# Both products of a convolutional feed-forward layer by one level of Strassen's recursion

## The chip, the core and the metric

The kernel runs on one core of a Trainium2 chip. The core has a matrix engine (PE), a vector engine (DVE), a scalar engine (ACT), a small general engine (POOL), a queue engine that issues transfers (SP), an on-chip memory of 128 partitions (SBUF) and eight accumulation banks of 128x512 float32 values (PSUM), which only PE writes. Each engine works through its own queue in order, and engines wait for each other by semaphores. The metric is the device time of one execution in microseconds (us), the median of three runs.

## The reference

One layer of a sequence model on x of 1024 tokens by 1024 features, in float32: a token mixer with two recurrences, then a gated feed-forward part, then a final norm. The change lies in the feed-forward part:

```python
def conv_ffn(h, up_w, conv_w, conv_b, down_w):      # h (1024, 1024), up_w (1024, 5632), down_w (2816, 1024)
    u = causal_dwconv(h @ up_w, conv_w, conv_b)      # causal convolution of width 3 along the tokens
    gate, val = jnp.split(u, 2, axis=-1)
    return (jax.nn.silu(gate) * val) @ down_w
...
x = x + gate_m * token_mixer(...)
h = rms_norm(x, ffn_norm_w) * (1.0 + scale_f) + shift_f
x = x + gate_f * conv_ffn(h, ...)
return rms_norm(x, final_norm_w)
```

## The kernel before

**Precision.** Each float32 operand of a large product is split into two parts of a shorter format, hi and lo (ACT copies hi, DVE subtracts to get lo), and a product is three matmuls: hi by hi, hi by lo, lo by hi. One matmul has a 128x128 stationary operand and 512 moving columns.

**The feed-forward part** keeps h transposed on chip (`hi_T`, `lo_T`: features on the partitions, 8 slabs of 128, by 1024 tokens). The 2816 hidden features are 22 slabs `f` of 128. `up_pair(f)` (L1182) makes one slab of the gate and one of the value: `feat_half` (L263) runs 24 matmuls (8 slabs of the inner dimension, 3 each) into one bank for 512 tokens, so a slab pair has 4 times 24 = 96 matmuls. Then ACT reads the bank twice (L1193: times the last tap, plus bias; L1194: a plain copy), DVE adds the other two taps (L1196), and `glu` (L1210) makes silu(gate)*value and splits it into hi and lo (L1216, L1218), which stay in SBUF. `down(gi)` (L1247) multiplies the slabs of a group of two or three (`GROUPS`) by their rows of `down_w`: for each of 8 token tiles 6 matmuls a slab, added to x in SBUF by DVE (L1270). Groups of ups and downs alternate; after the last group `final` (L1232) applies the final norm and writes the output.

**The order of the work** is written by the program itself: `run(gen)` steps a generator that issues PE work, a tick for every few matmuls, and `spawn` and `later` put the other engines' work a given number of ticks later; every queue then holds that order. Weights come through `Stream` (L155): SP loads 512 KB items into 4 raw buffers (`wraw`), ACT and DVE split them into 4 buffers each of `whi` and `wlo`, `ahead` keeps four items split and four loaded in front of the one in use.

**Before it**, the mixer runs its projections through `tok_block` (L242) and `feat_block`; HGRN2 heads (`hgrn_side`) share elementwise work between DVE and POOL. The last projection, `plan["out", n]` for the two halves n of the features, adds the gated result to x (`o_evac`, L1121), and in the second half `h2_tail` (L1148) makes h for one token tile at a time: POOL's power for the norm (L150), DVE's scaling (L1156), 8 transposes on PE (L379), the modulation on ACT and DVE, hi and lo.

Of the kernel before, what the change touches and what calls it, by code (L numbers as in the profile page):

```python
# [30 lines left out]
GROUPS = [2, 3, 3, 3, 3, 3, 2, 3]  # L31
# [25 lines left out]
def trunk(ctx, tc, x, c, ada_w, ada_b, mix_norm_w, in_w, in_b, mlstm_conv_w, mlstm_conv_b,  # L57
# [11 lines left out]
    vp = ctx.enter_context(tc.tile_pool(name="vp", bufs=1))  # L69
# [85 lines left out]
    class Stream:  # L155
# [24 lines left out]
        def split_hi(self):  # L180
# [4 lines left out]
            _, k, n, gain, work = self.items[i]  # L185
            t = self.raw.pop(i)[:, :k * n]
            if work is not None:
                work(t.rearrange("p (k n) -> p k n", k=k))
                return lambda: None
            if gain is not None:  # L190
                DVE.tensor_mul(t, t, gain())
# [50 lines left out]
    def tok_block(items, evac, ncols=512, before=None):  # L242
        segs = [(0, 512)] if ncols == 512 else [(0, 264), (264, 264)]
        for t in range(NT):
# [4 lines left out]
            for k in range(KD):  # L249
# [6 lines left out]
                if k % 2 == 1 and t == NT - 1:  # L256
                    st.after(items[k // 2], DEFER * (k // 2))
# [67 lines left out]

    def plan_heads(kind, hs):
# [18 lines left out]
    order, groups = [], []  # L345
    f0 = 0
    for gsz in GROUPS:
        groups.append(list(range(f0, f0 + gsz)))
        f0 += gsz
    for gi, fs in enumerate(groups):  # L350
        order += [("up", f) for f in (fs if gi == 0 else fs[1:])]
        if gi + 1 < len(groups):
            order.append(("up", groups[gi + 1][0]))
        order.append(("down", gi))
    for kind, i in order:
        if kind == "up":
            plan["ug", i] = feat_item(upw, i * P)
            plan["uv", i] = feat_item(upw, DFF + i * P)
        else:
            for f in groups[i]:  # L360
                plan["dn", f] = st.add([(0, D, downw[f * P:(f + 1) * P, :].unsqueeze(1))], 1, D,
                                       lambda: gates["f"])
# [172 lines left out]
    with tc.tile_pool(name="start", bufs=1) as sp:  # L535
# [6 lines left out]
        big = [vp.tile([P, 2, 2048], F32, name=n) for n in ("so", "v")]  # L542
# [87 lines left out]
        v_first = vp.tile([P, NT, 4, 129], F32, name="v")  # L630
# [338 lines left out]
    def mix_round(g, kind, v, prev_fin):  # L969
# [40 lines left out]
        so = R["so"] = vp.tile([P, NT, 512], F32, name="so")  # L1010
# [106 lines left out]
    x1h = [vp.tile([P, NT, 512], F32, name="v"), None]  # L1117
# [3 lines left out]
    def o_evac(n):  # L1121
        def sq(t, xt):
            ACT.activation(xt[:, 512:1024], x1h[n][:, t, :], AF.Square, accum_out=ss1[:, n, t:t + 1])

        xts = {}

        def xload(t):
            xts[t] = hdt([P, 1028], "pre" if t % 2 else "acc")
            SP.dma_start(out=xts[t][:, :512], in_=x2d[t * P:(t + 1) * P, n * 512:n * 512 + 512])

        def f(t, ps):
            if t == 0:
                xload(0)
            if t + 1 < NT:
                xload(t + 1)
            xt = xts[t]
            xv = x1h[n][:, t, :]
            DVE.tensor_mul(xv, ps[0], gates["m"][:, n * 512:n * 512 + 512])
            POOL.tensor_tensor(out=xv, in0=xv, in1=xt[:, :512], op=OP.add)
            if n == 0:  # L1140
                later(3, sq, t, xt)
            else:
                spawn(h2_tail(t, xt, sq), 3)
        return f

    h2_done = set()

    def h2_tail(t, xt, sq):  # L1148
        sq(t, xt)
# [4 lines left out]
        xn = hdt([P, 2 * S], "q")  # L1154
        for n in range(2):
            DVE.tensor_scalar(xn[:, n * 512:n * 512 + 512], x1h[n][:, t, :], rs1[:, t:t + 1], None,  # L1156
                              op0=OP.mult)
        yield H2[2]
        d = hdt([P, KD, P], "row" if t % 2 else "kt")
        modulate(t, d, gff, sff, [transposed(xn, hf) for hf in range(2)])  # L1160
        yield H2[3]
        modulate_lo(t, d)
        h2_done.add(t)

    run(tok_block(plan["out", 0], o_evac(0), before=lambda t: force(lambda: t in yt_done)))
    force(lambda: bool(fin_done))
    x1h[1] = vp.tile([P, NT, 512], F32, name="so")
    run(tok_block(plan["out", 1], o_evac(1)))

    mix.close()  # L1170
# [11 lines left out]
    def up_pair(f):  # L1182
# [4 lines left out]
        for pre in (pg, pv):  # L1187
            POOL.memset(pre[:, 0:2], 0.0)  # L1188
# [125 lines left out]
```

## Time and profile before

| what | value |
|---|---|
| time, median of 3 runs (lowest to highest) | 2010.45 us (2008.45 to 2013.41) |
| span of the profiled execution | 2008.3 us, 2.1 us under that median; the page has no other time of this execution |
| busy: PE, DVE, ACT, POOL | 1953.1, 1242.9, 658.0, 344.7 us |
| matmuls on PE | 9339, of them 2112 in the 22 slab pairs (L269) and 1056 in the downs (L1259) |
| first matmul of the downs, last matmul | 1334.7 us, 2000.4 us |
| bytes moved | 143.95 MB, 72 GB/s on average |

PE's busy time counts a matmul of 512 columns with 0.39 us although the next one starts 0.23 us later, so its share says that PE always has work, not that it could not be faster. The profile has a slice view (40 equal parts of the span), windows of any stretch, groups of instructions by line, a chain of waits followed back from the end, and a list of what an engine did in order of time.

### The profile page before, as it was taken

Reading aid. Unit: us, or ns where it says so; the run is one execution under the profiler, and the core shown is the slowest. Engines: PE = TensorE matmul, PEld = TensorE weight load, DVE = VectorE, ACT = ScalarE, POOL = GpSimd, SP = SyncE. Lnnn points to the kernel's source line nnn. Section 1 sums busy time; section 2 is a strip of 40 time slices with the busy share of each in tenths; the row PEclk is TensorE's granted clock in tenths of the full one; section 3 lists DMA queues with packets and bytes.
Section 4 is the critical chain, followed back from the end, with each engine's and each line's share of the span. In section 5 each row is a group of like instructions: output and inputs, shape, how many; then the busy total and the mean of one; then the engine's idle time right before and its main releaser. Section 6 shows DMA issues by size and latency. Waiting matters only on the chain.

```text
span 2008.3 us, 24395 instructions
## 1 busy us (share of the span) xinstructions
PE 1953.1 (97%) x9339; PEld 1629.4 (81%) x9339; DVE 1242.9 (62%) x2411; ACT 658.0 (33%) x1231; POOL 344.7 (17%) x485
## 2 busy tenths in 40 slices
PE   4999999999999999999999999999999999999998
PEld 4987888888887888888888778888888888888886
DVE  7676556677587474565675765765555555555656
ACT  3564432121313253321213133523232323232323
POOL 1211222124252022211243522100000000000000
PEclk9999999999999999999999999999999999999999
DMA  8232224121206222141102042211111212020202
GB/s 321 61 93 64 78 52 136 53 68 32 89 16 184 84 72 71 53 126 32 53 11 90 3 160 84 91 42 53 32 64 32 65 30 69 26 73 24 72 11 94
DMA packets 140965, 143.95 MB, mean 72 GB/s; under 512 B 6793, under 2 KB 109617, under 8 KB 139825
## 3 DMA queue, kind: packets, MB, share of 16 engines
q1 hardware_dynamic: 128640, 130.91, 20.5%
q10 hardware_dynamic: 12209, 11.49, 2.3%
q8 instruction: 73, 1.20, 0.2%
q14 instruction: 43, 0.35, 0.1%
HBM read 131.85 MB, written 10.53 MB: 71 GB/s over the span
## 4 chain that ended last, share of the span: by engine, by line
PE 84%; DVE 11%; ACT 1%; issue 1%; DMA 1%; POOL 1%; SPq 0%; DVEq 0%; POOLq 0%; ACTq 0%
PE mmb L269 39%; PE mmb L253 25%; PE sdb L1259 6%; PE mmb L1259 6%; DVE q L811 3%; DVE acc L808 2%; PE sdb L801 2%; DVE row L790 1%; PE sdb L741 1%; PE sdb L901 1%; DVE ada L573 1%; DVE wlo L199 1%; PE sdb L717 1%; PE sdb L885 1%; PE sdb L743 1%
## 5 line engine op out<-in xcount | busy, mean ns | idle before, releaser
L269 PE MATMUL mmb<-hiT,whi 128*128 128x512 f32 x1216 | 484.7, 399 | 0.0
L269 PE MATMUL mmb<-loT,whi 128*128 128x512 f32 x1216 | 477.3, 393 | 0.6 <-DVE loT L400 0.6
L269 PE MATMUL mmb<-hiT,wlo 128*128 128x512 f32 x1216 | 477.7, 393 | 0.0
L253 PE MATMUL mmb<-whi,hiT 128*128 128x512 f32 (+1 forms) x960 | 371.7, 398 | 1.3 <-ACT hiT L394 1.0
L253 PE MATMUL mmb<-whi,loT 128*128 128x512 f32 (+1 forms) x960 | 355.4, 381 | 3.3 <-DVE loT L957 2.9
L253 PE MATMUL mmb<-wlo,hiT 128*128 128x512 f32 (+1 forms) x960 | 354.1, 380 | 0.8 <-DVE wlo L199 0.8
L194 ACT ACTIVATE whi<-wraw 128x1024 fp32r<-128x1024 f32 (+1 forms) x154 | 162.6, 1060 | 435.7 <-PE mmb L1259 161.4
L199 DVE TENSOR_TENSOR wlo<-wraw,whi 128x1024 fp32r<-128x1024 f32 (+1 forms) x152 | 187.1, 1238 | 176.0 <-ACT whi L194 175.3
L269 PEld LDWEIGHTS mmb<-hiT,wlo 128*128 128x128 f32 x1216 | 228.9, 188 | 51.6 <-DVE wlo L199 0.2
L269 PEld LDWEIGHTS mmb<-loT,whi 128*128 128x128 f32 x1216 | 229.4, 189 | 49.4 <-DVE loT L400 1.0
L269 PEld LDWEIGHTS mmb<-hiT,whi 128*128 128x128 f32 x1216 | 229.3, 189 | 48.2
L253 PEld LDWEIGHTS mmb<-whi,loT 128*128 128x128 f32 x960 | 177.0, 189 | 39.6 <-DVE loT L957 3.3
L253 PEld LDWEIGHTS mmb<-whi,hiT 128*128 128x128 f32 x960 | 178.0, 190 | 31.1 <-ACT hiT L394 1.3
L253 PEld LDWEIGHTS mmb<-wlo,hiT 128*128 128x128 f32 x960 | 177.9, 190 | 31.0 <-DVE wlo L199 1.1
L1188 POOL MEMSET pre<- 128x2 f32 x22 | 2.2, 100 | 661.6 <-DVE acc L1213 660.8
L811 DVE TENSOR_TENSOR q<-q,row 128x128 f32<-128x128 f32 (+1 forms) x304 | 108.5, 408 | 1.7
L1196 DVE SCALAR_TENSOR_TENSOR kt<-pv,fcols,kt 128x512 f32<-128x512 f32 x84 | 63.2, 752 | 72.0 <-ACT pv L1194 70.5
L935 POOL TENSOR_TENSOR so<-so,ev 128x512 f32<-128x512 f32 (+3 forms) x64 | 67.6, 1056 | 231.3 <-ACT ev L933 230.1
L808 DVE COPY_PREDICATED acc<-lmask,sdb 128x128 f32<-128x128 uint8 (+2 forms) x320 | 99.8, 326 | 10.4 <-PE sdb L801 2.7
L801 PE MATMUL sdb<-q,pre 128*128 128x192 f32 x512 | 95.1, 327 | 7.3 <-DVE q L811 3.8
L801 PEld LDWEIGHTS sdb<-q,pre 128*128 128x128 f32 x512 | 85.2, 189 | 17.3 <-issue 5.2
L656 DVE SCALAR_TENSOR_TENSOR acc<-pre,bcols,acc 128x512 f32<-128x512 f32 x96 | 74.9, 780 | 19.5 <-ACT acc L667 17.6
(293 smaller groups left out, 2530.8 us busy)
## 6 DMA issues: line engine op xcount, KB each, us to landing
wraw<-in_in_w_dram SPq DMA_DIRECT2D x80, 512.0 KB
wraw<-in_ffn_up_w_dram SPq DMA_DIRECT2D x44, 512.0 KB
araw<-in_ada_w_dram SPq DMA_DIRECT2D x64, 256.0 KB
wraw<-in_ffn_down_w_dram SPq DMA_DIRECT2D x22, 512.0 KB
so<-in_ada_w_dram SPq DMA_DIRECT2D x4, 1024.0 KB
v<-in_ada_w_dram SPq DMA_DIRECT2D x4, 1024.0 KB
row<-bcdram ACTq DMA_DIRECT2D x8, 512.0 KB
ydram<-ev SPq DMA_DIRECT2D x16, 256.0 KB
```

The lines of the kernel that those rows point to most:

```text
L194: ACT.activation(hi[:, :k * n], t, AF.Copy)
L199: eng.tensor_tensor(out=lo[:, :k * n], in0=t, in1=hi[:, :k * n].bitcast(F32), op=OP.subtract)
L253: PE.matmul(b[:, :n], lhsT=a[:, k, ts], rhs=w[:, k % 2, o:o + n], start=(k == 0 and a is hi_T and w is whi), stop=(k == KD - 1 and a is lo_T))
L269: PE.matmul(ps, lhsT=w[:, k, :], rhs=a[:, k, hs], start=(k == 0 and w is whi and a is hi_T), stop=(k == KD - 1 and w is wlo))
L573: DVE.scalar_tensor_tensor(acc, slot(k), cs[:, k:k + 1], acc, op0=OP.mult, op1=OP.add)
L656: DVE.scalar_tensor_tensor(acc[:, hs], pre[:, o + tap:o + tap + 512], convw(tap, j), acc[:, hs], op0=OP.mult, op1=OP.add)
L801: PE.matmul(ps[:, i * 192:i * 192 + 192], lhsT=K[:, cc * P:(cc + 1) * P], rhs=cols(cc), start=True, stop=True)
L808: DVE.copy_predicated(o, mk.to_broadcast(list(d.shape)), d)
L811: e.tensor_tensor(out=o, in0=x, in1=y, op=OP.mult)
L935: POOL.tensor_tensor(out=so[:, t, r], in0=so[:, t, r], in1=g[:, r], op=OP.mult)
L1196: DVE.scalar_tensor_tensor(cnv[:, hs], pre[:, o + tap:o + tap + 512], fw(tap, j), cnv[:, hs], op0=OP.mult, op1=OP.add)
L1259: PE.matmul(pss[n], lhsT=a[:, ts], rhs=w[:, 0, n * 512:n * 512 + 512], start=(f == fs[0] and a is zhi[f] and w is dhi), stop=(f == fs[-1] ...
```

## The change

One level of Strassen's recursion (Winograd's form) splits each operand into 2x2 blocks and computes the product from 7 block products and 15 block sums instead of 8 block products. It is applied to both feed-forward products.

**Up.** h is split into 4 quarters (features by tokens), and `h2_tail` writes seven hi/lo quarters: a11, a12, a22 and the sums s1 to s4 (two sums on DVE and two on POOL a token tile, for the tiles 4 to 7; the lo parts of s3 and s4 on POOL). The token tiles of the second half of the output projection run in the order 0, 4, 1, 2, 5, 3, 6, 7. The slab pair of gate and value plays the two column blocks of the weights: `up_combine(f)` makes four sums of weight blocks on POOL. `up_head(f)` and `up_rest(f)` run 7 products of 12 matmuls into three banks x, y, w. Since x and w accumulate one product on top of another, ACT copies the bank to SBUF between two products (`snapped`, four times a slab pair), and the next product into that bank waits for the copy. The gate's tap and sigmoid, the value's taps (DVE) and the product gate times value (now on POOL) follow.

**Down.** The gated activations z are not kept in SBUF: for each pair j of slabs POOL makes four sums, and SP stores z and the sums to DRAM (`zd`, 1.75 MB a pair). The sums of the down weights are made during the mixer by `dn_combine` (11 rounds of 1 MB loaded, 4 sums on POOL, 1 MB stored to `td`). After all ups, seven phases of 11 steps run; a step loads 256 KB of z and 256 KB of weights, splits both, and runs 12 matmuls. Banks are copied by ACT (`snapshot`) or added by DVE between phases, x is read back from DRAM (`x1_dram`), and the gate, the residual and the final norm follow, in the last phase for the last token tiles one after another (`finish_last`).

```diff
-    def up_pair(f):
...
-            ACT.activation(pg[:, r], cg[:, r], AF.Sigmoid)
-            DVE.tensor_mul(cg[:, r], cg[:, r], pg[:, r])
-            yield 1
-            DVE.tensor_mul(cv[:, r], cv[:, r], cg[:, r])
-            ACT.activation(zh[:, r], cv[:, r], AF.Copy)
...
+    def dn_combine():
+        for j in range(NJ):
+            r = pw.tile([P, 2, D], F32, name="dnr")
...
+            combine(POOL, b11, b12, b11)
+            combine(POOL, b12, b22, b12)
+            yield 12
+            combine(POOL, b22, b22, b11)
+            combine(POOL, b21, b21, b22)
...
+    def combine(eng, o, x, y, op=OP.subtract):
+        eng.tensor_tensor(out=o, in0=x, in1=y, op=op)
...
+    def put(name, t, src, eng=DVE):
+        ts = slice(t % 4 * P, t % 4 * P + P)
+        h, l = (q[:, :, ts] for q in quarter[name])
+        ACT.activation(h, src, AF.Copy)
+        eng.tensor_tensor(out=l, in0=src, in1=h.bitcast(F32), op=OP.subtract)
...
+            combine(DVE, s1, d[:, 0:4], d[:, 4:8], OP.add)
+            combine(DVE, s2, s1, d0[:, 0:4])
+            combine(POOL, d[:, 0:4], d0[:, 0:4], d[:, 0:4])
+            put("s2", t, s2)
+            put("s3", t, d[:, 0:4], POOL)
+            put("s1", t, s1)
+            yield 2
+            put("a22", t, d[:, 4:8])
+            combine(POOL, d0[:, 4:8], d0[:, 4:8], s2)
+            put("s4", t, d0[:, 4:8], POOL)
...
+    def up_combine(f):
...
+        combine(POOL, tt[:, 0:4], uv[:, 0:4], ug[:, 0:4])
+        combine(POOL, tt[:, 4:8], uv[:, 4:8], tt[:, 0:4])
+        combine(POOL, uv[:, 0:4], uv[:, 4:8], uv[:, 0:4])
+        combine(POOL, t4, ug[:, 4:8], tt[:, 4:8])
...
+    def up_mm(f, bank, what, half, a, first=False, last=False):
...
+                PE.matmul(bank, lhsT=w[:, k, :], rhs=x[:, k, :], start=first and k == 0 and i == 0,
...
+    def snapped(bank):
+        s = up.tile([P, 512], F32, name="sn", bufs=3)
+        ACT.activation(s, bank, AF.Copy)
+        return s
...
+    def up_head(f):
...
+        yield from up_mm(f, x, "a", 0, "a11", first=True)
+        if f > 1:
+            snaps[f] = snapped(x)
+        yield from up_mm(f, y, "a", 1, "a12", first=True, last=True)
...
+        def gate(h):
+            ACT.activation(cg[:, half(h)], body(pg, h), AF.Identity, bias=fb(f), scale=fw(2, f))
+            yield 1
+            taps(pg, cg, f, h)
+            yield 2
+            ACT.activation(pg[:, half(h)], cg[:, half(h)], AF.Sigmoid)
+            yield 1
+            DVE.tensor_mul(cg[:, half(h)], cg[:, half(h)], pg[:, half(h)])
...
+        def value(h):
+            taps(pv, cv, NF + f, h)
+            POOL.tensor_tensor(out=cv[:, half(h)], in0=cv[:, half(h)], in1=cg[:, half(h)], op=OP.mult)
...
+        s1 = snaps.get(f) or snapped(x)
+        DVE.tensor_add(body(pg, 0), s1, y)
+        spawn(gate(0), 1)
+        yield from up_mm(f, x, "b", 1, "s2")
+        s2 = snapped(x)
+        yield from up_mm(f, w, "c", 0, "s3", first=True)
+        s7 = snapped(w)
+        yield from up_mm(f, x, "b", 0, "s1")
+        s4 = snapped(x)
+        POOL.tensor_tensor(out=body(pv, 1), in0=s4, in1=s7, op=OP.add)
+        yield from up_mm(f, w, "d", 0, "a22", last=True)
+        DVE.tensor_add(body(pg, 1), s2, w)
+        spawn(gate(1), 1)
+        ACT.activation(cv[:, half(1)], body(pv, 1), AF.Identity, bias=fb(NF + f), scale=fw(2, NF + f))
+        yield from up_mm(f, x, "c", 1, "s4", last=True)
+        ACT.activation(body(pv, 0), x, AF.Copy)
+        ACT.activation(cv[:, half(0)], x, AF.Identity, bias=fb(NF + f), scale=fw(2, NF + f))
...
+    run(up_head(0))
+    run(up_head(1))
+    force(lambda: len(h2_done) == NT)
...
+    run(up_rest(0))
+    prep(2)
+    run(up_rest(1))
...
+    steps = [[st.add([(0, 512, z_item(j, zi, zn)), (512, 512, src(j, i, n))], 1, D,
+                     ready=lambda j=j: j in z_done) for j in range(NJ)] for zi, zn, src, i, n in phases]
```

Three places show how the queues stand now. On ACT, in the middle of the ups, the rows of a slab pair before (acc and kt are the gate and the value behind the convolution, pre and pv their inputs, q the hi part of z):

```order
L1193 ACTIVATE acc<-mmb,fcols 128x512
L1194 ACTIVATE pre<-mmb 128x512
L1193 ACTIVATE kt<-mmb,fcols 128x512
L1194 ACTIVATE pv<-mmb 128x512
L1212 ACTIVATE pre<-acc 128x512
L1216 ACTIVATE q<-kt 128x512
L194 ACTIVATE whi<-wraw 128x1024
```

and now, from the first copy of a bank of slab pair f to its last sigmoid (sn is a copied bank, cg and pg the gate behind and ahead of the taps, L1329 the sigmoid, whi and whd hi parts of the next pair's weight blocks):

```order
L1292 ACTIVATE sn<-mmb 128x512
L1254 ACTIVATE whi<-wraw 128x1024
L1325 ACTIVATE cg<-pg,fcols 128x512
L1254 ACTIVATE whi<-tt 128x1024
L1329 ACTIVATE pg<-cg 128x512
L1292 ACTIVATE sn<-mmb 128x512 x2
L1254 ACTIVATE whd<-t_11813 128x512
L1292 ACTIVATE sn<-mmb 128x512
L1254 ACTIVATE whi<-wraw 128x1024
L1379 ACTIVATE cv<-pv,fcols 128x512
L1325 ACTIVATE cg<-pg,fcols 128x512
L1329 ACTIVATE pg<-cg 128x512
```

The copies of the banks are new, and the second and third of them (the sixth row) stand behind the sigmoid of the gate's first half.

On POOL, around the first slab pairs before (the last rows of `h2_tail`, the gate's row, and the zeros ahead of each convolution, which is all POOL has in the ups):

```order
L1139 TENSOR_TENSOR so<-so,pre 128x512
L1188 MEMSET pre 128x2
L1188 MEMSET pv 128x2
L150 TENSOR_TENSOR rs_9173<-rs_9173,nhalf 128x1
L966 TENSOR_TENSOR gf<-gf,k 128x1024
```

and now, in the ups, from the value of an odd slab pair to that of the next (L1375 the value from two copied banks, tt and t the weight sums, L1337 gate times value, s and s4z the sums of z, once for two slab pairs):

```order
L1375 TENSOR_TENSOR pv<-sn 128x512
L351 TENSOR_TENSOR tt<-wraw 128x512
L351 TENSOR_TENSOR tt<-wraw,tt 128x512
L351 TENSOR_TENSOR wraw<-wraw 128x512
L351 TENSOR_TENSOR t_12117<-wraw,tt 128x512
L1337 TENSOR_TENSOR cv<-cv,cg 128x512 x2
L351 TENSOR_TENSOR s_12142<-cv 128x512
L351 TENSOR_TENSOR cv<-cv 128x512
L351 TENSOR_TENSOR s_12142<-s_12142,cv 128x512
L351 TENSOR_TENSOR s4z<-cv,s_12142 128x512
```

POOL had no tensor work here, and now has 7 operations of 128x512 for one slab pair and 11 for the other.

On DVE, a slab pair's value and gate before, ahead of the lo part of z and of a weight item:

```order
L1196 SCALAR_TENSOR_TENSOR kt<-pv,fcols,kt 128x512 x2
L1213 TENSOR_TENSOR acc<-acc,pre 128x512
L1215 TENSOR_TENSOR kt<-kt,acc 128x512
L1218 TENSOR_TENSOR q<-kt,q 128x512
L199 TENSOR_TENSOR wlo<-wraw,whi 128x1024
```

and now, from the lo part of the last weight block to the taps of the next slab pair's gate:

```order
L1255 TENSOR_TENSOR wlo<-wraw,whi 128x1024
L1377 TENSOR_TENSOR pg<-sn,mmb 128x512
L1321 SCALAR_TENSOR_TENSOR cg<-pg,fcols,cg 128x512 x2
L1331 TENSOR_TENSOR cg<-cg,pg 128x512
L1321 SCALAR_TENSOR_TENSOR cv<-pv,fcols,cv 128x512 x4
L1255 TENSOR_TENSOR wlo<-wraw,whi 128x1024
L1314 MEMSET pg 128x2
L1367 TENSOR_TENSOR pg<-sn,sdb 128x512
L1321 SCALAR_TENSOR_TENSOR cg<-pg,fcols,cg 128x512 x2
```

The first sum of the next slab pair's gate (L1367) now stands behind the value's four tap operations of the pair before it and behind a weight split.

More of the change, by code (lines that the diff above doesn't have):

```diff
@@ L344, in trunk @@
     gates = {}
[L345 to L362, printed above, removed]
     bcols = consts.tile([P, 120], F32, name="bcols")
@@ L1221, in up_pair @@
[L1221 to L1234 removed]
+        def gate(h):
[6 more added lines that the diff above has]
+            DVE.tensor_mul(cg[:, half(h)], cg[:, half(h)], pg[:, half(h)])
+            if h == 1:
+                gate_done.add(f)
@@ new lines, in trunk, with down_mm, down_phase @@
+    xb = [mm_bank() for _ in range(4)]
+    def down_mm(w, bank, t, first=False, last=False):
+        h, l = st.get(w)
+        ts = slice(t * P, t * P + P)
+        for i, (a, b) in enumerate(((h, h), (h, l), (l, h))):
+            PE.matmul(bank, lhsT=a[:, 0, ts], rhs=b[:, 0, 512:1024], start=first and i == 0,
+                      stop=last and i == 2, skip_group_check=True)
+    def down_phase(ws, bk, first, last, hold=0):
+        n = NJ - hold
+        for j in range(n):
+            for t in range(4):
+                down_mm(ws[j], bk[t], t, first and j == 0, last and j == NJ - 1)
+                if t < 3:
+                    yield
+            st.ahead(ws[j])
+            yield
+        for t in range(4) if hold else ():
+            for j in range(n, NJ):
+                down_mm(ws[j], bk[t], t, False, last and j == NJ - 1)
+                if j < NJ - 1:
+                    yield
+            finish_last(t)
+            yield
@@ L1235, in final, with snapshot, add_out @@
+    def snapshot(name, bk):
+        s = dy.tile([P, 4, 512], F32, name=name)
+        for t in range(4):
+            ACT.activation(s[:, t, :], bk[t], AF.Copy)
+        return s
+    def add_out(t, n, c):
+        r = slice(n * 512, n * 512 + 512)
+        POOL.tensor_tensor(out=c, in0=c, in1=gates["f"][:, r], op=OP.mult)
+        POOL.tensor_tensor(out=xo[:, t, r], in0=xo[:, t, r], in1=c, op=OP.add)
+        yield 3
+        square(n, t, xo[:, t, r], c)
+    def final(t, end=False):
         DVE.tensor_add(rs1[:, t:t + 1], ss1[:, 0, t:t + 1], ss1[:, 1, t:t + 1])
@@ L1285, in trunk, with finish_last @@
-    for kind, i in order:
-        run(up_pair(i) if kind == "up" else down(i))
+            if end:
+                (SP, ACT)[n].dma_start(out=out2d[t * P:(t + 1) * P, r], in_=xo[:, t, r])
+        if not end:
+            SP.dma_start(out=out2d[t * P:(t + 1) * P, :], in_=xo[:, t, :])
+    def finish_last(t):
+        r = slice(512, 1024)
+        DVE.tensor_mul(tail[:, t % 2, :], xb[t], gates["f"][:, r])
+        DVE.tensor_add(xo[:, t, r], xo[:, t, r], tail[:, t % 2, :])
+        square(1, t, xo[:, t, r], tail[:, t % 2, :])
+        spawn(final(t, t == 3), 1)
@@ L1287, in trunk @@
+    spawn(g_c21(), 1)
+    tail = dz.tile([P, 2, 512], F32, name="gb")
+    run(down_phase(steps[6], xb, False, True, 4))
     force(lambda: not tasks)
```

424 lines of the change are left out of this document (289 added, 135 removed).

## The prediction

> **What bounds the kernel now.** First the page: engines and clock, then the chain of waits by engine.
>
> ```profile
> span 2008.3 us, 24395 instructions
> PE 1953.1 (97%) x9339; PEld 1629.4 (81%) x9339; DVE 1242.9 (62%) x2411; ACT 658.0 (33%) x1231; POOL 344.7 (17%) x485
> ...
> PEclk9999999999999999999999999999999999999999
> ...
> PE 84%; DVE 11%; ACT 1%; issue 1%; DMA 1%; POOL 1%; SPq 0%; DVEq 0%; POOLq 0%; ACTq 0%
> ```
>
> PE ends the chain for 84% of the span. The windows (length, then busy time and instructions of PE, PEld, DVE, ACT and POOL, granted clock, transfer share, GB/s) say how the feed-forward part stands, and the chain in order of time gives PE's pace:
>
> ```profile
> 1340.00:1400.00 60.00, 60.00 (x262) 48.84 (x261) 33.06 (x46) 17.18 (x25) 0.13 (x2) 1.00 0.15 46
> 1400.00:1600.00 200.00, 200.00 (x868) 162.76 (x867) 108.58 (x141) 61.68 (x90) 0.78 (x12) 1.00 0.16 48
> ```
>
> ```profile
> 1357.53 66.18 PE mmb L269 x288
> ...
> 1979.81 4.20 PE mmb L1259 x18
> ```
>
> There PE never waits, DVE is busy 54% of the time and POOL not at all. An up matmul takes 66.18/288 = 0.2298 us, a down matmul 4.20/18 = 0.2333 us. So here a matmul less is worth its time, as long as the work that replaces it stays beside PE.
>
> **What is saved.** Ups: 22 x (96 - 84) = 264 matmuls x 0.2298 = 60.7 us. Downs: 1056 - 7 x 11 x 12 = 132 x 0.2333 = 30.8 us. Together 91.5 us.
>
> **The new work, and a port.** A slab pair now takes PE 84 x 0.2298 = 19.3 us and brings POOL 7 or 11 operations of 128x512 in turn. What POOL and DVE do to each other stands in the lists by time:
>
> ```profile
> 482.15 1.16 DVE L811 TENSOR_TENSOR q<-q,row 128x256 f32<-128x256 f32 x4
> ...
> 485.68 3.17 DVE L811 TENSOR_TENSOR q<-q,row 128x256 f32<-128x256 f32 x4
> ```
>
> ```profile
> 486.30 0.91 POOL L931 TENSOR_TENSOR so<-ev 128x256 f32<-128x256 f32 x1
> 487.18 0.90 POOL L811 TENSOR_TENSOR pre<-pre,k 128x256 f32<-128x256 f32 x1
> ```
>
> ```profile
> 1262.38 2.00 DVE L199 TENSOR_TENSOR wlo<-wraw,whi 128x1024 fp32r<-128x1024 f32 x1 [0.44 <-ACT whi L194]
> ...
> 1268.42 1.22 DVE L199 TENSOR_TENSOR wlo<-wraw,whi 128x1024 fp32r<-128x1024 f32 x1
> ```
>
> ```profile
> 1262.02 1.27 POOL L1139 TENSOR_TENSOR so<-so,acc 128x512 f32<-128x512 f32 x1 [3.32 <-DVE so L1138]
> 1268.59 2.19 POOL L1139 TENSOR_TENSOR so<-so,pre 128x512 f32<-128x512 f32 x1 [3.32 <-DVE so L1138]
> ```
>
> ```profile
> 275.87 1.29 POOL L935 TENSOR_TENSOR so<-so,ev 128x512 f32<-128x512 f32 x1 [2.16 <-ACT ev L933]
> 275.88 0.69 DVE L718 TENSOR_TENSOR row<-row,sdb 128x512 f32<-128x512 f32 x1 [1.36 <-ACT ev L933]
> ```
>
> Alone, four DVE products take 1.16 us; with POOL working (485.55 to 488.7) they take 3.17, one POOL operation between each two. The 1024-wide subtraction takes 1.22 alone and 2.00 when it meets a POOL operation; POOL's 1.27 becomes 2.19 when DVE was first. The product with a PSUM input (sdb) keeps its 0.69 beside a POOL operation. So DVE operations with two SBUF inputs and POOL operations exclude each other and take turns; the one that waited saves about 0.14 of its start (1.27 becomes 1.14 behind the other's end). Taps, lo parts and products are all of that kind.
>
> **Two slab pairs on that port:** POOL 18 x 1.14 = 20.5 us; DVE, by the groups below less 0.14 each, 6 lo parts of 1024 columns (1.09), 16 taps (0.61), 6 others (0.55): 19.6. That makes 40.1 us, against 38.6 of PE: full even without a gap.
>
> ```profile
> L199 DVE TENSOR_TENSOR wlo<-wraw,whi 128x1024 fp32r<-128x1024 f32 x60 | 73.5, 1226 | 76.1 <-ACT whi L194 76.1
> L194 ACT ACTIVATE whi<-wraw 128x1024 fp32r<-128x1024 f32 x60 | 63.7, 1061 | 254.5 <-PE mmb L1259 161.4 <-PE mmb L269 77.4 <-DVE wraw L191 15.5
> L1196 DVE SCALAR_TENSOR_TENSOR kt<-pv,fcols,kt 128x512 f32<-128x512 f32 x84 | 63.2, 752 | 72.0 <-ACT pv L1194 70.5
> L1193 ACT ACTIVATE kt<-mmb,fcols 128x512 f32<-128x512 f32 x42 | 32.4, 771 | 73.1 <-PE mmb L269 73.1
> ...
> L1213 DVE TENSOR_TENSOR acc<-acc,pre 128x512 f32<-128x512 f32 x42 | 28.7, 684 | 0.0
> L1212 ACT ACTIVATE pre<-acc 128x512 f32<-128x512 f32 x42 | 26.4, 629 | 0.0
> L1194 ACT ACTIVATE pv<-mmb 128x512 f32<-128x512 f32 x42 | 24.8, 590 | 0.0
> ```
>
> ```profile
> L781 ACT ACTIVATE k<-k,lb,olb x16: 814/817/817, 335.6 to 1099.1; 128x512 f32<-128x512 f32 x16
> ```
>
> **The loop's chain.** The fifth product (s1) into bank x may start when ACT has copied x, and that copy stands on ACT behind the sigmoid of the gate's first half. Let 0 be the end of one fifth product; the next would start at 72 x 0.2298 = 16.54. Along the queues, without conflicts: copy of x and hi of the last weight block on ACT (0.59 + 1.06), its lo and the gate's sum on DVE (1.23 + 0.68), scale (0.82), two taps (1.50), sigmoid and the value's two reads on ACT (0.63 + 0.59 + 0.77), four taps (3.01), a weight's lo and the next gate's sum (1.23 + 0.68), scale (0.82), two taps (1.50), sigmoid and copy (0.63 + 0.59): 16.3, with hand-overs 16.5. It just fits, so every conflict is a stall of PE. POOL's value sum meets the lo part (+0.2); the four weight sums follow it and meet the gate's two taps (+1.5); gate times value meets the value's last tap (+1.1). That is 19.25, a stall of 2.7. After each second slab pair the z sums also meet the next gate's taps (+1.7): 4.4. Behind that copy ACT holds the copy of w and the small hi part, for which the next products wait too, but later. Bounds: 0 (no meeting) and 10 (each of POOL's 9 operations a round, 1.14, holds up the chain). I take the walk: 10 x 2.7 + 10 x 4.4 = 71 us for slab pairs 2 to 21. Slab pair 1 has its first 24 matmuls behind it, so only 60 x 0.2298 = 13.8 us cover a round of 22: 8.2. On SP the stores of z wait for POOL's sums ahead of the next weight loads, but those are read two slab pairs later: nothing.
>
> **The clock.** What a stall does to it, in windows of the old mixer:
>
> ```profile
> 1162.00:1163.00 1.00, 0.00 (x0) 0.00 (x0) 1.00 (x5) 0.53 (x1) 0.00 (x0) 1.00 0.61 193
> ...
> 1166.00:1167.00 1.00, 1.00 (x4) 0.74 (x3) 1.00 (x3) 0.00 (x0) 0.00 (x0) 0.50 0.95 336
> 1167.00:1168.00 1.00, 1.00 (x6) 0.80 (x5) 0.96 (x7) 0.63 (x1) 0.16 (x1) 0.50 0.78 281
> ...
> 1169.00:1170.00 1.00, 1.00 (x7) 0.83 (x6) 1.00 (x2) 0.64 (x2) 0.92 (x2) 1.00 1.03 385
> ...
> 1110.00:1112.00 2.00, 0.00 (x0) 0.00 (x0) 1.93 (x9) 0.00 (x0) 0.00 (x0) 1.00 0.00 0
> 1112.00:1114.00 2.00, 1.79 (x10) 1.78 (x11) 1.93 (x7) 0.00 (x0) 0.00 (x0) 1.00 0.00 0
> ```
>
> After a gap of 2.9 us the granted clock was 0.50 for some 3.4 us; after one of 2.4 us it stayed at 1.00. Of the five gaps of 2 to 3 us in the trace three were followed by half speed. Half speed for 3.4 us costs 1.7, and it falls into the product that the next round starts from. 22 stalls x 0.6 x 1.7 = 22 us; bounds 0 and 37. The Trainium skill (TensorE: Matmul & The Clock Gate, Part 1) lets the clock drop after an idle window of about 3.4 us; by it only the longer stalls would count, 11 x 1.7 = 19. The trace has drops after 2.0 us.
>
> **Into the ups.**
>
> ```profile
> PE mmb L269 <- DVE loT L400: 0.6, 1, 0.6
> ```
>
> ```profile
> 1267.82 0.69 DVE L1138 TENSOR_TENSOR so<-mmb,k 128x512 f32<-128x512 f32 x1
> ```
>
> ```profile
> 1271.99 0.55 POOL L150 TENSOR_TENSOR rs<-rs,nhalf 128x1 f32<-128x1 f32 x1 [0.27 <-DVE rs L149]
> ```
>
> ```profile
> 1275.28 1.03 PE L379 MATMUL sdb<-ident,q 128*128 128x128 f32 x8
> ```
>
> Before, PE waits 0.6 us for the last tile of h. PE's cover behind the last output product is 48 up matmuls (11.0) and two sets of transposes (2 x 1.03): 13.1 us, now as then. Counted from that product's end (0), the new walk is: product, POOL's sum of x, square, then hi and lo parts of slab pair 0's blocks, whose source buffers the next sums overwrite: 5.9. POOL's four weight sums (5.1) stand ahead of its power (0.55): 11.5. Scaling, with one meeting, and transposes: 14.7. The tile before has five DVE and four POOL operations in turns, then comes the last tile's modulation: 21.4. Its two sums and lo of s2: 25.2. POOL's lo of s3 and sum of s4: 27.6; hi of s4 and, behind it on ACT, the first bank copy: 28.9. So the second product of slab pair 0 is 15.8 late, 15.2 more than before. Bounds 0 and 25 (as much again for the tile before).
>
> **The rest.** Mixer: 44 POOL sums x 1.14, of which the 11% of the chain that is DVE's counts: 5 us (0 to 50, if every one counted). Downs: a step lasts 12 x 0.2333 = 2.8 us and needs ACT 1.06 and DVE 1.23, so the splits hide, as long as loads come: 512 KB a step is 187 GB/s, and 417 while x and three rows come too (5.8 MB in 25 us).
>
> ```profile
> GB/s 0 59 296 392 400 413 413 426 419 419 446 439 419 354 419 419 419 426 419 360 269 388 390 405 413 401 393 328 346 268 11 72 143 175 300 375 330 125 333 54
> ```
>
> The first 50 us held about 415, so I take 2 us (0 to 10), the wait for the last z included. The Trainium skill (SBUF — State Buffer, A bandwidth-pool intuition) gives HBM 358 GB/s; by it 1.5 MB would run late, 4 us. At the end one product more and DVE's queue: 2 us (0 to 4).
>
> **The sum:** -91.5 + 71 + 8.2 + 15.2 + 22 + 5 + 2 + 2 = +34 on the span of 2008.3, so 2042.3; the median of the runs lies 2.1 above the span: **2044 us**, slower by 1.7%.
>
> **The rivals.** *Stalls, but the clock holds* (gaps between dense matmuls, like that at 1110): 22 less, 2022 us. *Faster, POOL slips into DVE's pauses:* the chain leaves DVE idle while ACT works (6.5 us a round), and where the weight sums fall into it, a stall shrinks to about 1.8, under the shortest gap with a drop: -91.5 + 36 + 4 + 8 + 6 = -37, 1973 us. Against it: the weight sums are released just ahead of the taps. *No conflict at all:* -91.5 + 8 = 1927 us; the rows at 485.68 speak against it. *Loads too slow in the downs:* if 300 GB/s held, as for some slices above, the 5.8 MB would add 10 us to the forecast: 2054 us.
>
> **How the numbers follow.** Forecast 0.42 (its own range 2025 to 2068), clock holds 0.18, POOL slips in 0.30, no conflict 0.04, loads 0.06. Below 1965 and above 2068 I leave 0.1 each. A measurement here tells 0.3% (6 us). Slower: 0.48 and most of the second, 0.59; the same 0.07; faster 0.34.
>
> **What would show it.** In the ups: rounds of 23 to 25 us instead of 19.3; PE waiting at its fifth product for ACT's copy; taps with a mean of 1.2 us or more instead of 0.75, POOL's 128x512 operations above 1.27; a granted clock below 0.95. Ahead of them a gap of about 15 us, and no PE waits in the downs. Wrong would be a round near 20 us with full clock, waits in the downs, or a mixer longer by more than 15 us.

## The result and the profile after

The changed kernel takes 2093.36 us (median of 4 runs, 2092.97 to 2093.67) against 2011.68 us for the kernel before (4 runs on the same chip): a ratio of 1.0412, 95% interval 1.0397 to 1.0427. It is slower by 4.1%, where 1.7% was forecast: the sign was right, the time lies above the range (up to 2068). The profiled execution spans 2091.2 us, 82.9 more than the span before.

The page of the changed kernel, with busy times, the clock by slices and the chain of waits by engine:

```profile
span 2091.2 us, 24544 instructions
PE 1917.8 (92%) x8943; PEld 1588.5 (76%) x8943; DVE 1375.5 (66%) x2367; ACT 753.1 (36%) x1336; POOL 809.6 (39%) x727
...
PEclk9999999999999999999999998799999998999998
...
PE 55%; DVE 25%; ACT 8%; issue 5%; POOL 4%; DMA 3%; SPq 0%; ACTq 0%; POOLq 0%; DVEq 0%
```

PE's part in the chain fell from 84% to 55%; DVE, ACT and POOL now end 37% of the span. PE has 396 matmuls fewer, as the change says. What it waited for, from the list of waits (engine and line, what it waited for: us in all, times, longest):

```profile
PE mmb L1286 <- ACT sn L1292: 55.5, 12, 11.1
PE sdb L1286 <- ACT sn L1292: 27.3, 11, 4.7
...
PE mmb L1286 <- ACT hiT L1190: 7.8, 1, 7.8
...
PE sdb L388 <- DVE row L1203: 7.4, 2, 5.1
...
PE mmb L1463 <- DVE wlo L203: 5.7, 2, 4.3
```

In the ups PE waits 82.8 us for a bank copy `sn` on ACT (L1292), more than for all else there. (The first two rows are one kind of wait: odd and even slab pairs use different banks, `mmb` and `sdb`.) The chain of waits of the changed kernel in order of time, from ahead of one such wait to behind the next, shows why the copy is late:

```profile
1521.39 1.21 DVE wlo L1255
1522.60 0.62 DVE pg L1367
...
1523.25 0.83 ACT cg L1325
...
1524.10 1.57 DVE cg L1321
...
1525.69 1.65 DVE cg L1321
...
1527.42 0.63 ACT pg L1329
1528.05 0.49 ACT sn L1292
...
1528.59 5.50 PE mmb L1286 x12
...
1544.66 1.43 DVE cv L1321 x2
...
1546.17 1.52 issue
1547.69 1.22 DVE wlo L1255
...
1553.20 3.02 PE sdb L1286 x12
```

From one product s1 to the next, 1528.59 to 1553.20, the chain passes PE only for 5.5 us. The 1.52 us of "issue" at 1546.17 are DVE's fourth tap, which waits for nothing that the profile names: POOL's product runs there. The same two taps of the gate show the port in the list by time, once with the z sums on POOL and once without:

```profile
1524.10 3.23 DVE L1321 SCALAR_TENSOR_TENSOR cg<-pg,fcols,cg 128x512 f32<-128x512 f32 x2 [0.89 <-ACT cg L1325]
1525.19 1.59 POOL L351 TENSOR_TENSOR cv<-cv 128x512 f32<-128x512 f32 x1
1526.74 1.71 POOL L351 TENSOR_TENSOR s<-s,cv 128x512 f32<-128x512 f32 x1
1528.59 0.80 PE L1286 MATMUL mmb<-hiT,whi 128*128 128x512 f32 x1 [4.19 <-ACT sn L1292]
...
1550.40 1.54 DVE L1321 SCALAR_TENSOR_TENSOR cg<-pg,fcols,cg 128x512 f32<-128x512 f32 x2 [0.89 <-ACT cg L1325]
```

**Where the 82.9 us are**, by the starts and ends of PE's work in the two traces:

| part | measured against before | forecast |
|---|---|---|
| 396 matmuls | -91.5 | -91.5 |
| mixer and output projection, up to the last output product (ends 1285.6, before 1266.3) | +19.2 | +5 |
| from there to the second product into bank x of slab pair 0 (s2; "second product" below): 39.5 us instead of 13.7 (a cover of 13.1 and a wait of 0.6) | +25.8 | +15.2 |
| rest of the ups: 531.1 us for 1800 matmuls of 0.2298 (413.6) | +117.5 | +101.2 (71 + 8.2 + 22) |
| downs: 223.7 us for 924 matmuls of 0.2333 (215.6) | +8.1 | +2 |
| behind the last matmul: 11.4 us instead of 7.5 | +3.9 | +2 |
| sum (the rounded rows make 83.0) | +82.9 | +34 |

### The profile page after: what moved, and what is told of

Read it like the earlier page. It is cut to its first block, busy times and chain, and to the rows that moved or that the text cites. A ratio compares the mean times of both kernels' runs of the same rounds, so it can differ in the third digit from the quotient of the medians.

```text
span 2091.2 us, 24544 instructions
## 1 busy us (share of the span) xinstructions
PE 1917.8 (92%) x8943; PEld 1588.5 (76%) x8943; DVE 1375.5 (66%) x2367; ACT 753.1 (36%) x1336; POOL 809.6 (39%) x727
## 4 chain that ended last, share of the span: by engine, by line
PE 55%; DVE 25%; ACT 8%; issue 5%; POOL 4%; DMA 3%; SPq 0%; ACTq 0%; POOLq 0%; DVEq 0%
PE mmb L257 22%; PE mmb L276 13%; DVE cg L1321 5%; PE mmb L1463 4%; PE sdb L1463 3%; PE sdb L1286 3%; PE mmb L1286 3%; DVE q L822 3%; DVE wlo L1255 3%; DVE cv L1321 2%; DVE acc L819 2%; PE sdb L812 2%; DVE row L801 2%; ACT cg L1325 2%; ACT pg L1329 1%
## 5 line engine op out<-in xcount | busy, mean ns | idle before, releaser
L203 DVE TENSOR_TENSOR wlo<-wraw,whi 128x1024 fp32r<-128x1024 f32 (+1 forms) x163 | 211.7, 1311 | 186.8 <-ACT whi L198 186.1
L276 PE MATMUL mmb<-hiT,whi 128*128 128x512 f32 x512 | 208.9, 408 | 0.0
L276 PE MATMUL mmb<-hiT,wlo 128*128 128x512 f32 x512 | 202.0, 394 | 0.8 <-DVE wlo L203 0.8
L276 PE MATMUL mmb<-loT,whi 128*128 128x512 f32 x512 | 201.5, 394 | 0.0
L1321 DVE SCALAR_TENSOR_TENSOR cg<-pg,fcols,cg 128x512 f32<-128x512 f32 x88 | 119.0, 1352 | 38.0 <-ACT cg L1325 36.5
L1337 POOL TENSOR_TENSOR cv<-cv,cg 128x512 f32<-128x512 f32 x44 | 85.3, 1940 | 83.6 <-DVE cv L1321 83.0
L1255 DVE TENSOR_TENSOR wlo<-wraw,whi 128x1024 fp32r<-128x1024 f32 x44 | 60.9, 1383 | 83.2 <-ACT whi L1254 83.1
L276 PEld LDWEIGHTS mmb<-hiT,wlo 128*128 128x128 f32 x512 | 96.8, 189 | 23.4 <-DVE wlo L203 1.2
L276 PEld LDWEIGHTS mmb<-loT,whi 128*128 128x128 f32 x512 | 97.3, 190 | 19.2
L276 PEld LDWEIGHTS mmb<-hiT,whi 128*128 128x128 f32 x512 | 97.2, 190 | 18.9
L1286 PE MATMUL mmb<-hiT,whi 128*128 128x512 f32 x132 | 62.2, 471 | 51.3 <-ACT sn L1292 43.5
```

Source lines behind the costliest of these rows:

```text
L203: eng.tensor_tensor(out=lo[:, :k * n], in0=t, in1=hi[:, :k * n].bitcast(F32), op=OP.subtract)
L276: PE.matmul(ps, lhsT=w[:, k, :], rhs=a[:, k, hs], start=(k == 0 and w is whi and a is hi_T), stop=(k == KD - 1 and w is wlo))
L1255: DVE.tensor_tensor(out=l, in0=src, in1=h.bitcast(F32), op=OP.subtract)
L1286: PE.matmul(bank, lhsT=w[:, k, :], rhs=x[:, k, :], start=first and k == 0 and i == 0, stop=last and k == 3 and i == 2, skip_group_check=True)
L1321: DVE.scalar_tensor_tensor(cnv[:, half(h)], pre[:, o:o + 512], fw(tap, j), cnv[:, half(h)], op0=OP.mult, op1=OP.add)
L1337: POOL.tensor_tensor(out=cv[:, half(h)], in0=cv[:, half(h)], in1=cg[:, half(h)], op=OP.mult)
```

## The experiments

The "port" is the exclusion that the prediction read from the trace: DVE operations with two SBUF inputs and POOL operations take turns; a "meeting" is one of them waiting for the other. Three accounts stood against each other. **Chain:** the bank copies stand in ACT's queue behind work that waits for DVE, so that everything which lengthens DVE's part, meetings on the port above all, stops PE. **Meetings:** only the exclusion of DVE and POOL makes the stall, whatever the order. **Capacity:** the port is full, and no order helps. All runs below are single ones but the last two; runs with the same mixer differ in the end of the output projection by up to 5 us (1284.3 to 1289.2), so stages are compared by their own length. A round is the time of one slab pair.

### The first sigmoid behind the bank copies

```diff
-            yield 2
+            yield 11 if h == 0 else 2
             ACT.activation(pg[:, half(h)], cg[:, half(h)], AF.Sigmoid)
```

> The sigmoid of the gate's first half goes behind the third bank copy on ACT; everything else stays. Chain theory (a bank copy late on ACT stops PE): the cycle from the copy of the second product to the same copy one slab pair later no longer holds that sigmoid and the gate's two taps ahead of it; I add up 20.8 us for it (from durations in the changed kernel's trace), so rounds of about 21 us instead of 24.6, PE gaps of 1 to 1.5 us, and 2020 to 2030 us. Rival, port capacity (DVE and POOL together are full whatever the order): the round stays at 24 or more and the time within 10 us of 2093.

Measured: 2068.9 us, the round 23.5 instead of 24.7. One row moved on one queue took 24.5 us off, so the order counts. But the gain is a third of what I had added up: part of the stall moved to another product, whose copy stands behind the other sigmoid and the value's two reads. From the list by time:

```profile
1441.52 0.63 ACT L1329 ACTIVATE pg<-cg 128x512 f32<-128x512 f32 x1 [3.30 <-DVE cg L1321]
1442.06 0.58 ACT L1381 ACTIVATE pv<-mmb 128x512 f32<-128x512 f32 x1
...
1442.53 0.77 ACT L1382 ACTIVATE cv<-mmb,fcols 128x512 f32<-128x512 f32 x1
1443.19 0.59 ACT L1292 ACTIVATE sn<-sdb 128x512 f32<-128x512 f32 x1
...
1443.84 1.22 PE L1286 MATMUL sdb<-so,whi 128*128 128x512 f32 x2 [2.54 <-ACT sn L1292]
```

### POOL's sums left out

First the z sums alone, then the weight sums from slab pair 2 on as well.

```diff
-            combine(POOL, s12[:, 0], z0[:, half(1)], z1[:, half(1)], OP.add)
-            combine(POOL, z0[:, half(1)], z0[:, half(0)], z0[:, half(1)])
...
+            SP.dma_start(out=zd[j][2], in_=z1)
```

> The four sums of z after each second slab pair are left out on POOL; z itself is stored in their place, so the transfers stay. Port theory: only the odd gap shrinks, from 4.2 to the even pairs' 2.4 us, 10 x 1.8 = 18 us and up to 10 us of clock: 2065 to 2075. Rival (the odd gap comes from something else than these sums, such as the order of the banks): both gaps stay, 2093.

> As the run without z sums, and from slab pair 2 on the four weight sums are left out too (raw blocks are used in their place), so POOL keeps only the value's sum and the two products of gate and value. Port theory: the gate's taps of the second half fall from 3.3 to 1.5 us, both gaps to 0.5 us or less, rounds near 20, the clock stays at 1.00: about 2000 us. Rival (the chain of hand-overs is too long even without meetings): gaps of 2 us and more stay, 2045 or more.

Measured: 2074.1 and 2011.6 us. Without z sums the wait of every second round fell from 4.2 to 2.5 us, the others stayed at 2.4: the odd stall is those four sums. Without the weight sums too the waits are 0.7 and 0.8 us and the round is 20.5; expected were 0.5 us or less and about 2000 us. In the window from 1400 to 1700 us, the groups of DVE for the gate's taps (mean ns in the middle, idle time behind), of the changed kernel, then without z sums, then without weight sums too:

```profile
L1321 DVE SCALAR_TENSOR_TENSOR cg<-pg,fcols,cg 128x512 f32<-128x512 f32 x50 | 68.6, 1372 | 23.0 <-ACT cg L1325 22.2
```

```profile
L1321 DVE SCALAR_TENSOR_TENSOR cg<-pg,fcols,cg 128x512 f32<-128x512 f32 x51 | 59.8, 1173 | 23.9 <-ACT cg L1325 23.0
```

```profile
L1324 DVE SCALAR_TENSOR_TENSOR cg<-pg,fcols,cg 128x512 f32<-128x512 f32 x58 | 43.6, 752 | 26.7 <-ACT cg L1328 25.7
```

So a tap costs 752 ns without meetings, as before the change. The rest of the result matters as much: with the loop nearly free of stalls the kernel still needs the time of the one before. The rest of the ups still takes 37.8 us more than its matmuls (117.5 in the changed kernel); the other 54 of the 91.5 us are spent around it.

### Order alone, engines alone, both

The order: both sigmoids, the value's products, the z sums and the preparation of the next weights are issued later; the value's taps keep their place, both halves at once.

```diff
-            yield 2
+            yield 12 if h == 0 else 7
             ACT.activation(pg[:, half(h)], cg[:, half(h)], AF.Sigmoid)
...
         def finish():
-            yield 1
+            yield 7
             value(0)
...
-            spawn(store(), 1)
+            spawn(store(), 7)
...
-        spawn(g(), 1)
+        spawn(g(), 9)
```

The engines: the weight sums, the value's sum, gate times value and the z sums run on DVE.

```diff
-            POOL.tensor_tensor(out=cv[:, half(h)], in0=cv[:, half(h)], in1=cg[:, half(h)], op=OP.mult)
+            DVE.tensor_tensor(out=cv[:, half(h)], in0=cv[:, half(h)], in1=cg[:, half(h)], op=OP.mult)
```

> Order alone: in the loop over slab pairs both sigmoids, the two products of gate and value, the z sums and the preparation of the next pair's weights are issued later, so that no bank copy on ACT stands behind work that waits for DVE; POOL keeps all its sums. By a walk along the queues with the measured durations and the port rule (DVE operations with two SBUF inputs and POOL operations take turns), the port itself is then what is left: two pairs need 40 us of it and get it with holes, so rounds of about 22 us, 2035 to 2050. Rival (the order is all there is to it, the port has room): rounds of 19.5 to 20, about 1990.

> Engines alone: every POOL sum and product of the loop from slab pair 2 on goes to DVE in the place where it is issued now; the order of everything else stays. POOL is idle, so nothing can meet on the port. Chain theory: DVE's queue gets longer between the value's taps and the gate's, which the bank copies wait for: rounds of 25 to 26, 2095 to 2125, slower than the change itself. Rival (the meetings on the port make the stall, whatever the order): the stalls go as in the run without sums, 2005 to 2020.

> Order and engines together: the late sigmoids and preparation of the order run with DVE doing the sums and products of the engine run. By the same walk the round is PE's own 19.3 us without a gap: 20 x 5.3 us less than the change, about 1987 us (1980 to 2000). Rival (effects that add: order alone minus what engines alone cost): 2060 or more.

Measured: 2040.6, 2114.2 and 1988.1 us; rounds of 22.0, 25.6 and 19.4. All three are where the chain account put them, and each rival fell. The windows from 1400 to 1700 us of the changed kernel, of order alone, engines alone and both (length, busy time of PE, PEld, DVE, ACT and POOL, granted clock, transfers):

```profile
1400.00:1700.00 300.00, 259.36 (x1017) 205.19 (x1015) 214.93 (x210) 125.95 (x184) 187.54 (x109) 0.91 0.25 81
```

```profile
1400.00:1700.00 300.00, 278.66 (x1148) 221.11 (x1147) 252.21 (x231) 139.24 (x205) 201.71 (x121) 0.97 0.28 92
```

```profile
1400.00:1700.00 300.00, 246.93 (x979) 196.00 (x978) 215.83 (x303) 120.08 (x175) 0.00 (x0) 0.90 0.24 78
```

```profile
1400.00:1700.00 300.00, 300.00 (x1297) 243.42 (x1297) 275.92 (x400) 159.89 (x230) 0.00 (x0) 1.00 0.32 104
```

With engines alone nothing can meet (POOL has 0 instructions) and the kernel is 21 us slower than the change, with waits of 3.0 and 5.9 us: meetings are not needed for the stall, a longer DVE queue between two bank copies is enough. The order alone still stalls at 1.1 and 2.1 us, with POOL on the port; together they make DVE 92% busy and PE never wait in this window. The two edits don't add: -53 and +21 make -105.

### The mixer's down weight sums

The four POOL sums of a round are left out, the transfers kept.

> In the mixer, the 44 sums of down weights are left out on POOL; loads and stores stay (the output projection starts with the same transfers). If POOL's sums hold up the mixer: its 12 us come back, about 2082 us. If the transfers do: 2093.

Measured: 2082.9 us; the last output product starts at 1274.56 instead of 1285.17. The 44 sums cost 10.6 us, 0.24 each; the transfers little. (Single runs: against the others with this mixer it is 9 to 14 us. Ahead of the last output block this run is 0.9 us behind the kernel before, the changed kernel 11.4.) From 300 to 600 us PE started 1448 matmuls before the change, 1414 behind it and 1451 without the sums. The windows of the changed kernel, then of the run:

```profile
300.00:600.00 300.00, 290.67 (x1414) 245.18 (x1413) 212.90 (x533) 64.16 (x124) 109.88 (x152) 0.99 0.29 93
600.00:700.00 100.00, 95.75 (x449) 78.56 (x448) 59.61 (x103) 26.71 (x52) 26.10 (x21) 0.98 0.45 140
```

```profile
300.00:600.00 300.00, 294.03 (x1451) 248.30 (x1450) 212.68 (x540) 65.82 (x133) 97.71 (x143) 1.00 0.30 94
600.00:700.00 100.00, 99.46 (x479) 82.45 (x478) 59.49 (x112) 32.70 (x65) 12.06 (x12) 1.00 0.48 149
```

### Into the ups

```diff
-            combine(POOL, d[:, 0:4], d0[:, 0:4], d[:, 0:4])
+            combine(DVE, d[:, 0:4], d0[:, 0:4], d[:, 0:4])
...
-            put("s4", t, d0[:, 4:8], POOL)
+            put("s4", t, d0[:, 4:8])
```

> Into the ups: the sums of h for s3 and s4 and their lo parts go from POOL to DVE, and the weight sums of slab pair 1 are issued after the first slab pair's second product. The loop stays as it is. If POOL's backlog and the waits of DVE and ACT behind it make the late start: the way from the last output product to the second product of slab pair 0 falls from 39.5 us to 25 to 30, the stall ahead of the last output products (5.1 us) shrinks too, 2073 to 2082. If DVE is the bound there, the longer DVE queue costs as much: 2090 or more.

Measured: 2090.9 us. The wait ahead of the last output products fell from 5.1 to 2.8, the way to the second product only from 39.5 to 36.5 (from the modelled end of the last output product, as in the table; the expectations below count from 0.2 us earlier). Expected were 25 to 30, so this theory of the way was wrong, and the time is that of its rival, DVE as the bound. The list by time of the run, a scaling alone, the late read, and the scaling beside POOL's weight sums:

```profile
1292.52 0.48 DVE L1203 TENSOR_SCALAR kt<-acc,rs 128x512 f32<-128x512 f32 x1
...
1294.12 0.68 DVE L1153 TENSOR_TENSOR pre<-mmb,k 128x512 f32<-128x512 f32 x1
...
1302.00 2.15 POOL L351 TENSOR_TENSOR tt<-wraw,tt 128x512 f32<-128x512 f32 x1
1302.93 1.50 DVE L1203 TENSOR_SCALAR row<-row,rs 128x512 f32<-128x512 f32 x1
1304.11 1.45 POOL L351 TENSOR_TENSOR wraw<-wraw 128x512 f32<-128x512 f32 x1
1304.35 1.50 DVE L1203 TENSOR_SCALAR row<-pre,rs 128x512 f32<-128x512 f32 x1
```

DVE reads the last output product 9.3 us after its end, because its queue holds the work of the two token tiles before and two weight splits; it idles for only 1 us of that. And POOL's weight sums, issued later but free to start, began at 1300.6 us (1300.9 in the changed kernel) and now met the scaling (1.50 instead of 0.48 us): a POOL operation that is moved back in the program isn't later in time if nothing stands ahead of it. Both edits stand in one run, so what each is worth isn't shown.

### All together

The loop of "both"; the sums of h and slab pair 1's weight sums on DVE; in the downs the gate, the residual and a sum of copied banks on DVE, and the final norm of a token tile behind the next tile's first operations. The second run also packs the mixer's eleven rounds of sums (211 to 992 us in the changed kernel) closer together; meant was the stretch from 690 to 950 us, in its trace they ran from 629 to 886.

```diff
-        POOL.tensor_tensor(out=xo[:, t, r], in0=xo[:, t, r], in1=c, op=OP.add)
+        DVE.tensor_tensor(out=xo[:, t, r], in0=xo[:, t, r], in1=c, op=OP.add)
...
-        spawn(final(t, t == 3), 1)
+        spawn(final(t, t == 3), 1 if t == 3 else 5)
```

> The order and engines of the two-part run (1988 us), with the sums of h on DVE and slab pair 1's weight sums on DVE too (no POOL work beside DVE behind the last output product), and in the downs the gate, the residual and the sum of two copied banks on DVE instead of POOL, the final norm of a token tile issued behind the next tile's first two operations. Port theory: the way from the last output product to the second product falls from 36.7 us (sums of h moved, POOL still summing weights) to about 32; the waits of the downs for a lo part (1.2, 0.8, 4.3 and 1.3 us, with half clock behind) go, and the tail shortens by 3 to 4 us: about 1966 us (1960 to 1975). Rival (DVE's queue is the bound in both places): 1980 or more.

> As the run before it, and the eleven rounds of down weight sums in the mixer are packed into the stretch from about 690 to 950 us, where the changed kernel fell no further behind (its lag stayed at 10.2 us there while four rounds ran). If the place of the sums decides: up to 9 us less than the run before it, about 1958. If each POOL sum costs its 0.24 us wherever it stands: the same time as the run before it; if the density hurts: more.

Measured: 1976.6 and 1966.8 us. The first missed by 10 and lies between its range and its rival's: the way to the second product came to 35.0 (not 32), the waits of the downs halved (7.7 to 4.0 us) instead of going, and behind the last matmul 11.4 us are left (13.0 in the run of both). The second gained 9.8, of which the mixer's end shows 5.0; another 1.8 lie in the way to the second product and 2.8 in the rest of the ups, which that edit doesn't touch, so up to half of the gain isn't explained by the place of the sums.

Two last runs, five rounds each, took the weight splits behind the last output products later, and then moved the mixer's sums once more.

```diff
     def first_prep():
-        yield 2
+        yield 1
+        up_split(1, "a")
+        yield 9
         up_split(0, "b")
```

> As the run with the packed down sums (1966.8 us), and behind the last output products the splits of weight blocks stand later: the second pair's first block behind the last token tile's product, the sums' blocks behind that tile's scaling instead of ahead of it. If the weight splits on DVE and ACT hold up the last token tiles (the last product's read was 11 us late, five weight splits stood ahead of the last tile's sums): the way to the second product falls from 33.5 us to 29 to 31, 1961 to 1965 us. If the chain of the token tiles themselves is the bound: unchanged, 1966 to 1969.

> As the run timed in five rounds (1965.9 us), but the eleven rounds of down weight sums begin 52 ticks later (behind the start of the third mixer round, where that run fell 5.7 us back at 643 us of the kernel before) and stand closer, 23 ticks apart instead of 30. If the place decides: the 5.7 us at 643 go, the 3 to 5 us lost by 794 stay or grow a little, 1959 to 1963. If the closeness hurts as much as the place helps: 1964 to 1970.

Measured: **1965.86 us** (1965.3 to 1969.7), a ratio to the kernel before of 0.9788 (0.9774 to 0.9801), and 1970.25 us, ratio 0.9810 (0.9797 to 0.9824). The first is the best version, 2.1% faster than the kernel before; the way to the second product stayed at 33.5 us (33.3 in the run before it), so the weight splits don't hold it up, and the chain of the token tiles remains the likeliest bound, not shown by a run. The second run, 0.2% longer with an interval that overlaps the first's, says what the mixer's sums ask for: with 23 ticks a round no time is lost around 643 us any more, but between 700 and 960 us PE starts 1209 matmuls, against 1266 in the run before it and 1285 in the changed kernel. The windows of this last run:

```profile
600.00:700.00 100.00, 99.52 (x471) 82.19 (x470) 66.82 (x118) 32.74 (x59) 24.89 (x22) 1.00 0.59 187
700.00:960.00 260.00, 250.01 (x1209) 207.04 (x1208) 169.72 (x328) 80.38 (x164) 101.85 (x90) 0.99 0.43 135
```

By the end of the output projection this run is 4.7 us behind the one before it. Place and closeness changed together, so that closeness cost more than the place gave is the likeliest reading and not shown by itself.

## Why the prediction was wrong

**Right: what is saved, and the mechanism of the loop.** 396 matmuls, the port, the copy behind the sigmoid, the fifth product as the place, and stalls of 2.4 and 4.2 us against 2.7 and 4.4 forecast. The rounds of 24.7 us, the taps' mean of 1.37 and the clock of 0.91 lie where they were looked for. The stalls come to 67 us against 71 in slab pairs 2 to 21 and to 4.7 against 8.2 in slab pair 1 (with the 11.1 ahead of the loop, the 82.8 above): these two terms were a little too large. Order alone, engines alone and both came out where the same walk put them.

**Wrong: the clock's share.** I let 0.6 of the stalls drop the clock, at 1.7 us. The windows of one stall of the changed kernel:

```profile
1524.50:1528.50 4.00, 0.00 (x0) 0.00 (x0) 3.96 (x3) 1.59 (x4) 3.87 (x3) 0.88 0.22 89
1528.60:1534.00 5.40, 5.40 (x13) 4.29 (x14) 3.22 (x3) 0.94 (x2) 2.07 (x1) 0.50 0.96 339
```

The starts of the matmuls behind a stall show half speed after 17 of 18 stalls of the steady rounds, at 1.4 to 2.7 us each, 1.7 on the mean over all 18: for 22 rounds 38 us instead of 22, at the upper bound given (37). The 0.6 came from three of five gaps of 2.0 to 2.9 us in the mixer, and was put on stalls of 4.2 us too. By the grid in the last section, an estimate from the traces, a gap of 2.4 us at a random place drops the clock in 6 of 10 cases and one of 4.2 always; here the short ones did it 8 times in 9 as well. The rival "the clock holds" fell.

**Wrong: the start of the walk into the ups.** "Counted from that product's end (0): product" took DVE to read the last output product at once; before the change the read began 1.5 us behind its end, now 10.2 us behind. The last output product, its read, the end of the weight sums, the power, and the copy that PE waits for, in the list by time of the changed kernel:

```profile
1285.17 0.39 PE L257 MATMUL mmb<-whi,loT 128*128 128x512 f32 x1
...
1295.79 0.69 DVE L1153 TENSOR_TENSOR pre<-mmb,k 128x512 f32<-128x512 f32 x1
...
1305.15 2.24 POOL L351 TENSOR_TENSOR t<-wraw,tt 128x512 f32<-128x512 f32 x1
1307.35 0.54 POOL L158 TENSOR_TENSOR rs<-rs,nhalf 128x1 f32<-128x1 f32 x1
...
1324.41 0.58 ACT L1292 ACTIVATE sn<-mmb 128x512 f32<-128x512 f32 x1
```

From the read on the walk holds (29.2 us to the end of the copy, 28.9 forecast). The step forgot that the three token tiles ahead bring the same extra work, so the engines come to this point with a backlog: +10.6, nearly all of it the late read. That the backlog is that of the token tiles is read from the queue; no run shortened it to 25 to 30 us.

**Wrong: the mixer,** and by more than the 15 us that I had named as a sign of it. "44 POOL sums x 1.14, of which the 11% of the chain that is DVE's counts": measured 10.6 for the sums. The share of an engine in the chain before says how often it is late, not what happens when it gets slower at a place where it almost is. Of the other 8.6 of this row 7.9 lie in the last output block (192 matmuls in 57.3 us instead of 49.4), where a wait of 5.1 us for the scaling, with half clock behind it, was in no term at all.

**Wrong, smaller.** Downs +8 (forecast 2, bounds 0 and 10): not the loads, which ran at 399 GB/s in the busiest stretch without a wait of PE, but the lo parts behind the final norms of the token tiles, 4.3 us at once. I had expected no waits there. The end +3.9 instead of 2. Some 8 us of the loop's row I can't place; in the run of both a round without a stall takes 19.4 us instead of 19.3, which would be 3 of them.

Five of seven costs were too small: the mixer's and the downs' were taken near the lower end of their bounds, the other three near the middle, because each by itself looked coverable. The bounds held them nearly all (the way into the ups ended at 25.8 against 25, the clock at 38 against 37), but the range let only a few of them come true together; a shared cause, engines that become late together, is the likeliest reason. "POOL slips into DVE's pauses", given 0.30, spoke for the other side and was far off: no stall shrank to the 1.8 us that it needed, those of the steady rounds stayed near 2.4 and 4.2.

## What to carry to other kernels

Work that is added to an engine beside a saturated PE is not paid in its own time: follow the copy that frees a PSUM bank along its queue, and see what each entry ahead of it waits for. Here order and engine had to be changed together; either alone recovered half or made it worse. Estimate the shared cause once and let all terms move with it, and start a walk at a stage's border with the backlog of the stage before it.

## What the runs showed of the hardware

**Gaps that drop the clock.** Over the 157 stalls (0.3 us and more) of slab pairs 3 to 20 in eight traces, those of the changed kernel and of the seven runs whose loop stalls, half speed followed none of 48 gaps under 2.0 us, 7 of 12 between 2.0 and 2.2, 47 of 52 between 2.2 and 2.6, and all 45 above; a drop cost 1.5 us, 2.1 behind gaps of 3.5 to 4.5. So a stall of 2.3 us mostly costs 3.8 and a shorter one only itself. The length of the gap is not all: in the slab pairs around these, one gap of 1.94 us was followed by half speed (engines alone) and one of 3.38 was not (first sigmoid). What settles it is where the gap lies. In each of these traces every change of the granted clock lies on a grid with steps of 3.41 us. Of the 959 steps of these loops that began at full clock, all 106 in which no matmul ran for 1.86 us or more were followed by half speed, and none of the 853 with 1.81 us or less (ends of matmuls as modelled). The five gaps of the old mixer part in the same way: the two that kept the clock, of 2.0 and 2.4 us, lie across the border of two steps. The Trainium skill (TensorE: Matmul & The Clock Gate, Part 1) has the clock drop after an idle window of about 3.4 us, and a window that runs freely. The grid fits a free window of that length; but a window need not be idle throughout, a little over half of it was enough in these traces.

**A scaling with one SBUF input meets POOL too.** The 128x512 TENSOR_SCALAR took 0.48 us alone and 1.50 beside POOL's sums, so more than the operations with two inputs take turns. The Trainium skill (SBUF — State Buffer, Who interferes with whom) says this of `tensor_scalar` in its two-port mode; the rows agree, though no run here shows the mode.
